# First layer's seven-product heads: softmax normalised one product later, fifth product ahead of the fourth, its weight sum by an adding load, single items

## The chip, the cores and the metric

The kernel runs on one core of a Trainium2 chip. The core has five engines that run their own queues of instructions: PE (matmuls), ACT (activations, copies, casts), DVE (elementwise work and reductions), POOL and SP, both of which also issue DMAs. The metric is the device time in us of one execution, the median of several.

## The reference

A decoder trunk of two layers over 512 tokens of width 2048, all in float32. The first layer is the sparse attention that the change is about; the second (stick-breaking attention, 16 heads) is left as it is.

```python
def _dsa_mixer(x, pos, w_in, w_out):
    h = x @ w_in
    q, k, v, g, qi, wi, ki = _split(h, A_SPLITS)
    ...
    dots = jnp.einsum('bqhd,bsd->bqhs', qib, ki)
    score = jnp.einsum('bqhs,bqh->bqs', jax.nn.relu(dots), wib)
    _, sel = lax.top_k(score, k_top)
    ...
    s = jnp.einsum('bqgrd,bqkgd->bqgrk', qg, ks) * scale
    pr = jax.nn.softmax(jnp.where(valid, s, -jnp.inf), axis=-1)
    o = jnp.einsum('bqgrk,bqkgd->bqgrd', pr, vs)
    return (o * jax.nn.silu(g)) @ w_out
```

It has 16 heads of 128 in 4 key/value groups and 16 indexer heads of 64, rope on q, k, qi and ki, and 128 selected keys per query. Each layer then does x = LayerNorm(alpha x + mixer(x)) and x = x + (p W) sigmoid(x G).

## The kernel before

**Tiles and chunks.** Activations are held transposed (features on the 128 partitions, 512 tokens along them). Weights come in chunks of 512 KB (128 x 1024). Each float32 operand is split into a high part, which ACT casts, and a low part, which DVE subtracts, and a product is made of three passes on PE: high by high, high by low, low by high. For weights these are wh (`split_w`, L370) and wl (L371); chunk c is split two steps ahead of its matmuls. There are six raw buffers and three pairs of split ones.

**Seven products.** `quads` (L210 on) makes the query and the gate of one head with seven half-width products, P1 to P7, after Strassen's scheme. Of the first layer's 16 heads, 0 to 2 are made plainly and 3 to 15 in 13 quads, numbered 0 to 12. One product is one chunk: its weights are a loaded block or a sum of blocks. A sum is made by an adding DMA from POOL's queue (`add_load`, L354) or by an add on DVE (`add_plus`, L359). Before the change P7 and P5 have adding loads, P6 and P4 have adds on DVE (P4's weights are P6's plus P2's). ACT copies partial results out of PSUM (L237 after P7, L241 after P1, L245 after P6, L273 after P3), DVE adds the others (L249 after P2, L255 after P5, L259 after P4). P6 accumulates in the bank of P1, so it starts when L241 has been done. P4 completes the head's query, P3 (of the quad before, run after the next quad's P1) its gate. The activations have forms of their own for P1 to P7; S1 and S4 are made late (`late_form`, `more_forms`), and the halves' sums come from `x_sums` during the chunks ahead of the quads.

**What sets the order.** Nothing schedules: the program's order is the order on each engine. `Kernel.run` walks the chunks; at each it splits weights of a chunk two steps ahead, runs the matmuls, then pops items from a queue (`pop`): `ch.pops` items, one by default, none after P5 and P3 in the first layer's quads. An item that is None counts as popped only where fewer than three items are left behind it. `soon` puts a function on a second list that is run at the next step, whatever `pops` is.

**Attention of the first layer.** Its items per head are, in `slots`: `turn` (rope of the query: three copies on ACT, L554 to L556; a multiplication on POOL, L557; two operations on DVE, L558 and L561; then a split, L109 and L110), `first` (value matmuls of the head before, then scores and softmax of query tiles 0 and 1), `second` (tiles 2 and 3), an empty item, and `last` (transposes of the probabilities by PE, L715, and their splits). `soft_tile` makes scores on PE (L125 to L127), mask and row maximum on DVE (L787), its negative (L789), the exponential with the row sum on ACT (L790), the reciprocal on DVE (L791) and, when both tiles of the item are so far, the normalisation on ACT (L795). The sparse selection comes before: relus of rough scores (L610) and 16 rounds on DVE (`top_rounds`), the mask (`mask_scores`) and the bias (`make_bias`) as items ahead and behind.

**The end of the stage.** The last softmaxes run as items of the output projection's chunks (`mix_out(0)`), two items a chunk in the first six.

## Time and profile before

| | us |
|---|---|
| time, median of 3 runs | 2155.71 (2153.93 to 2156.15) |
| the profiled execution's own time | 2154.26 |
| its span, first to last instruction | 2152.5 |
| PE busy | 2059.7 |
| DVE busy | 1729.5 |
| ACT busy | 1202.4 |
| POOL busy | 239.3 |
| ACT, cast of weights (L370), 552 times | 574.5 |
| DVE, subtraction for weights (L371), 552 times | 673.6 |
| DVE, sum of weights (L359), 126 times | 153.4 |

The indexer's part runs from about 100 to 279 us, quads 0 to 12 from there to 681 us, the output projection of the first layer after them. How to read the rows: a timeline row has start, duration, engine, line, operation, output<-input with shapes, and in brackets the idle time of the engine before it with what ended it. A row of waits has the total, the count and the longest. A window's row has the window, its length, the busy time of each engine with the number of instructions, the granted clock of PE, the busy share of the DMA engines and GB/s.

### The profile page before, as it was taken

How to read it: one execution, taken by the hardware profiler on the slowest of the kernel's cores; microseconds unless marked ns; L12 is line 12 of the kernel's file. 1: busy time of each engine (PE TensorE's matmuls, PEld its weight loads, DVE VectorE, ACT ScalarE, POOL GpSimd, SP SyncE). 2: the span in 40 equal slices, each digit the busy share in tenths (PEclk: the TensorE clock that was granted, in tenths of full speed). 3: DMA queues.
4: the chain of work that ended last, by engine and by line, in shares of the span. 5: the costliest groups of instructions: out<-in, count | busy, mean ns of one | idle time of the engine just before them, and what ended most of it. 6: DMA issues, size and time to landing. Idle time of an engine off the chain costs nothing. (4 is left out here: it accounts for less than half of the span.)

```text
span 2152.5 us, 33632 instructions
## 1 busy us (share of the span) xinstructions
PE 2059.7 (96%) x12808; PEld 1869.5 (87%) x12808; DVE 1729.5 (80%) x2692; ACT 1202.4 (56%) x1946; POOL 239.3 (11%) x323
## 2 busy tenths in 40 slices
PE   9988978889998899999999999999999999999999
PEld 7877868788887699889988888888888888998899
DVE  5687986667677689888788888888888888998886
ACT  4564345666666454655555555555555554546553
POOL 5201010101110000000001111111111110000000
PEclk9999999999999899999999999999999999999999
DMA  6532434435454256545745554655555574665354
GB/s 240 186 108 78 127 74 114 125 105 133 128 148 163 77 144 190 171 127 157 247 126 133 135 163 133 152 157 148 156 128 155 148 209 149 156 180 175 122 168 136
DMA packets 105905, 316.00 MB, mean 147 GB/s; under 512 B 11664, under 2 KB 16016, under 8 KB 105744
## 3 DMA queue, kind: packets, MB, share of 16 engines
q1 hardware_dynamic: 87600, 247.80, 33.1%
q0 software_dynamic: 18144, 66.07, 17.8%
q8 instruction: 100, 1.64, 0.3%
q14 instruction: 61, 0.50, 0.1%
HBM read 290.75 MB, written 23.07 MB: 146 GB/s over the span
## 5 line engine op out<-in xcount | busy, mean ns | idle before, releaser
L371 DVE TENSOR_TENSOR wl<-raw,wh 128x1024 fp32r<-128x1024 f32 (+1 forms) x552 | 673.6, 1226 | 174.1 <-ACT wh L370 173.4
L370 ACT CAST wh<-raw 128x1024 fp32r<-128x1024 f32 (+1 forms) x552 | 574.5, 1048 | 148.1 <-DVE raw L359 38.2
L201 PE MATMUL g<-f,wh 128*128 128x512 f32 x1680 | 423.7, 394 | 0.5 <-DVE f L120 0.5
L204 PE MATMUL g<-h,wh 128*128 128x256 f32 x1584 | 398.4, 288 | 19.4 <-ACT s L241 18.7
L204 PE MATMUL g<-l,wh 128*128 128x256 f32 x1584 | 396.1, 287 | 0.0
L201 PEld LDWEIGHTS g<-f,wh 128*128 128x128 f32 x1680 | 302.6, 189 | 56.4 <-DVE f L120 0.9
L204 PEld LDWEIGHTS g<-h,wh 128*128 128x128 f32 x1584 | 309.6, 195 | 22.9 <-ACT s L241 20.3
L204 PEld LDWEIGHTS g<-l,wh 128*128 128x128 f32 x1584 | 310.1, 196 | 0.8
L125 PE MATMUL g<-h,wh 128*128 128x512 f32 (+1 forms) x752 | 289.3, 385 | 5.2 <-ACT wh L370 5.2
L127 PE MATMUL g<-h,wl 128*128 128x512 f32 (+1 forms) x752 | 288.6, 384 | 2.1 <-DVE wl L371 2.1
L126 PE MATMUL g<-l,wh 128*128 128x512 f32 (+1 forms) x752 | 288.6, 384 | 0.3 <-DVE l L110 0.3
L207 PEld LDWEIGHTS g<-f,wl 128*128 128x128 f32 x1680 | 228.8, 190 | 18.4 <-DVE wl L371 2.2
L207 PE MATMUL g<-f,wl 128*128 128x256 f32 x1680 | 234.6, 282 | 0.8 <-DVE wl L371 0.8
L207 PE MATMUL g<-h,wl 128*128 128x256 f32 x1584 | 224.5, 285 | 1.9 <-DVE wl L371 1.9
L207 PEld LDWEIGHTS g<-h,wl 128*128 128x128 f32 x1584 | 206.6, 194 | 2.1 <-DVE wl L371 2.1
L125 PEld LDWEIGHTS g<-h,wh 128*128 128x128 f32 x752 | 143.4, 191 | 30.5 <-ACT wh L370 5.8
L127 PEld LDWEIGHTS g<-h,wl 128*128 128x128 f32 x752 | 143.0, 190 | 28.0 <-DVE wl L371 3.3
L126 PEld LDWEIGHTS g<-l,wh 128*128 128x128 f32 x752 | 143.1, 190 | 25.8 <-DVE l L110 0.9
L359 DVE TENSOR_TENSOR raw<-raw,raw 128x1024 f32<-128x1024 f32 x126 | 153.4, 1218 | 0.2
L280 ACT COPY s<-g 128x512 f32<-128x512 f32 x120 | 70.1, 584 | 100.9 <-PE g L207 100.8
L354 POOL DMA_DIRECT2D raw<-in_w_q_dram x60 | 53.0, 1032 | 413.3 <-issue 252.8
L109 ACT CAST h<-s 128x512 fp32r<-128x512 f32 (+1 forms) x124 | 60.4, 544 | 52.2 <-DVE s L987 38.2
(260 smaller groups left out, 2868.8 us busy)
## 6 DMA issues: line engine op xcount, KB each, us to landing
raw<-in_w_out_dram SPq DMA_DIRECT2D x64, 512.0 KB, 4.3
raw<-in_w_gate_dram SPq DMA_DIRECT2D x64, 512.0 KB, 3.8
raw<-in_w_q_dram SPq DMA_DIRECT2D x64, 512.0 KB, 4.8
raw<-in_w_q_dram POOLq DMA_DIRECT2D x60, 512.0 KB, 6.3
raw<-in_w_kv_dram SPq DMA_DIRECT2D x56, 512.0 KB, 4.4
raw<-in_w_qa_dram SPq DMA_DIRECT2D x52, 512.0 KB, 3.7
raw<-in_w_in_dram SPq DMA_DIRECT2D x45, 512.0 KB, 4.0
raw<-in_w_qa_dram POOLq DMA_DIRECT2D x26, 512.0 KB, 5.7
```

What stands on the lines that cost most here:

```text
L109: nc.scalar.copy(h[:, lo:w], src[:, lo:w])
L125: nc.tensor.matmul(out, ah, bh, start=start, stop=False)
L126: nc.tensor.matmul(out, ah, bl, start=False, stop=False)
L127: nc.tensor.matmul(out, al, bh, start=False, stop=stop)
L201: nc.tensor.matmul(ps, part(ch.h, j), x[0], start=first, stop=False, skip_group_check=True)
L204: nc.tensor.matmul(ps[:, :HALF], part(ch.h, j), x[n], start=first and n == 0, stop=False, skip_group_check=True)
L207: nc.tensor.matmul(ps[:, :HALF], part(ch.l, j), x[0][:, :HALF], start=False, stop=stop and j == last, skip_group_check=True)
L280: nc.scalar.copy(q[name], q[bank])
L354: self.nc.gpsimd.dma_start(ch.raw, ch.add, accum_op=OP.add)
L359: self.nc.vector.tensor_tensor(ch.raw, ch.raw, ch.plus.raw, op=OP.add)
L370: nc.scalar.copy(ch.h[:, i:i + w], ch.raw[:, i:i + w])
L371: nc.vector.tensor_tensor(ch.l[:, i:i + w], ch.raw[:, i:i + w], ch.h.bitcast(F32)[:, i:i + w], op=OP.subtract)
```

## The change

Six edits, all in the first layer or in code that it shares with the second.

1. In `quads`, with `late4` (first layer alone), P5 is run ahead of P4, and P4's weights are made by an adding load of the raw block onto P6's, instead of by an add on DVE.
2. Softmax: the masked scores are scaled by a negative factor and DVE takes the minimum, which the exponential uses with scale -1, so the multiplication by -1 is gone. Reciprocals and normalisation of a pair of tiles are put on `soon`, so they come after the next product (`stage_t` does them if they are still to be done).
3. Items: `slots` has [rope of this head if it is still to be done, tiles 0 and 1, tiles 2 and 3, rope of the next head, transposes]; a rope item that finds nothing to do returns False, and `pop` then goes on to the next item if three or more are left.
4. Pops: the last chunk of the keys has one pop (none before), chunks 27 and 28 one (two before), the first six output chunks one (two before). The selection's mask and bias are part of the first and last of the 16 rounds' items.
5. `x_sums` puts the split of its sum on `soon`.
6. The late forms: S4 has a tile of its own, S1 goes into the second halves of the tiles of x; S1 is made behind P1, P7 and P6 in the first layer's quads, S4 behind P5, P4 and P7.

```diff
...
         while n > 0 and self.queue and (force or self.queue[0][0] < self.now):
             fn = self.queue.pop(0)[1]
             if fn:
-                fn()
+                fn = fn() is not False
             if fn or len(self.queue) < 3:
                 n -= 1
...
-    def quads(self, sources, forms, done, copied=False, lanes=False):
+    def quads(self, sources, forms, done, copied=False, lanes=False, late4=False):
...
             q["B"] = None
         def after5(q):
-            if q["n"] == len(sources) - 1:
+            if q["n"] == len(sources) - 1 and not late4:
                 nc.scalar.copy(q["o2"][:, :HALF], q["A"][:, :HALF])
             nc.vector.tensor_tensor(q["o2"][:, HALF:], q["s17"][:, HALF:], q["A"][:, :HALF], op=OP.add)
             q["s17"] = None
         def after4(q):
             nc.vector.tensor_tensor(q["o1"][:, HALF:], q["o2"][:, :HALF], q["E"][:, :HALF], op=OP.add)
+            if q["n"] == len(sources) - 1 and late4:
+                nc.scalar.copy(q["o2"][:, :HALF], q["A"][:, :HALF])
             q["E"] = None
             done(q["n"], 0, q["o1"])
             q["o1"] = None
...
                 third(last)
             product(q, "P6", "S2", "A", False, False, after6, grown=q["P7"], plus=q["P1"])
             product(q, "P2", "A12", "B", True, True, after2, fresh=(1, c1))
-            product(q, "P4", "A22", "E", False, True, after4, grown=q["P6"], plus=q["P2"])
+            if not late4:
+                product(q, "P4", "A22", "E", False, True, after4, grown=q["P6"], plus=q["P2"])
             product(q, "P5", "S1", "A", False, False, after5, add=(0, c2), grown=q["P1"])
+            if late4:
+                product(q, "P4", "A22", "E", False, True, after4, grown=q["P6"], add=(1, c1))
...
         rope(ps, st[2], 32, lambda a: qidx.__setitem__(m, stacked(a)), col=P)
         k.defer_by(1, lambda: idx_pair(m, 3, "ss"), lambda: (idx_pair(m, 2, "ss"), idx_pair(m, 1, "so")))
         if m == 7:
-            k.defer(mask_scores)
             for r in range(0, 16):
-                k.defer(lambda: [top_rounds(b, 1) for b in range(1, NT)])
-            k.defer(make_bias)
+                k.defer(lambda r=r: (mask_scores() if not r else None, [top_rounds(b, 1) for b in range(1, NT)],
+                                     make_bias() if r == 15 else None))
...
     def tail(h, a):
         def stage_t():
+            if "normal" in a:
+                normals(a)
             a["pt"] = []
             banks = [k.ps("s") for _ in range(3)]
             where = {0: (0, 0), 1: (1, 0), 3: (1, 384), 2: (2, 0)}
...
             if h % 4 == 0:
                 v_load(h // 4)
-        def turn():
+        def turn(h):
+            a = att.get(h, ())
+            if "t" not in a:
+                return False
             if h % 4 == 0:
                 k_load(h // 4)
             rope(a.pop("t"), st[0], 64, lambda r: a.__setitem__("q", k.split(r)))
-        if h >= PLAIN_A:
-            k.defer(turn)
-        k.defer(first, second, None, last)
+        k.defer(lambda: turn(h), first, second, lambda: turn(h + 1), last)
         if h == HEADS - 1:
             k.defer(lambda: pending.pop()())
...
     def soft_tile(a, i):
         ps, n = scores(a, i)
-        pr, mx, sm = k.tt(s="pr"), k.small(), k.small()
-        nc.vector.tensor_tensor_reduce(pr[:, :n], ps[:, :n], bias[i][:, :n], scale=SCALE, scalar=GONE, op0=OP.add,
-                                       op1=OP.max, accum_out=mx)
-        nc.vector.tensor_scalar(mx, mx, -1.0, None, op0=OP.mult)
-        nc.scalar.activation(pr[:, :n], pr[:, :n], AF.Exp, bias=mx, scale=1.0, accum_out=sm)
-        nc.vector.reciprocal(sm, sm)
+        pr, mn, sm = k.tt(s="pr"), k.small(), k.small()
+        nc.vector.tensor_tensor_reduce(pr[:, :n], ps[:, :n], bias[i][:, :n], scale=-SCALE, scalar=-GONE, op0=OP.add,
+                                       op1=OP.min, accum_out=mn)
+        nc.scalar.activation(pr[:, :n], pr[:, :n], AF.Exp, bias=mn, scale=-1.0, accum_out=sm)
         a["p"][i] = pr
         def normal():
+            nc.vector.reciprocal(sm, sm)
             nc.scalar.activation(pr[:, :n], pr[:, :n], AF.Identity, scale=sm)
-        return normal
+        a.setdefault("normal", []).append(normal)
+
+    def normals(a):
+        for fn in a.pop("normal", ()):
+            fn()
     def soft_tiles(a, *tiles):
-        for fn in [soft_tile(a, i) for i in tiles]:
-            fn()
+        for i in tiles:
+            soft_tile(a, i)
+        k.soon(lambda: normals(a))
...
     for g in range(0, KV_A, 2):
         k.block(w_in, 26 + 2 * g, xs, lambda i, ps, g=g: k_done(g + i, ps))
         k.chunks[-1].pop_first = False
-        k.chunks[-1].pops = 0
     k.chunks[12].then(v_store)
     for h in range(PLAIN_A):
         k.block(w_in, 34 + 4 * h, xs, lambda i, ps, h=h: q_done_a(h, i, ps))
...
     def x_sums(j):
         a, b = xsum[j]
         sums_in_place(a, b)
-        x23[j] = k.split(a)
         xsum[j] = b
+        k.soon(lambda: x23.__setitem__(j, k.split(a)))
     def x_more(name, js):
         for j in js:
-            if j not in x14:
-                x14[j] = k.tt(F32R, "x14")
-            late_form(name, xT[2 * j], xsum[j], x14[j])
+            late_form(name, j, xT[2 * j], xsum[j], x14)
             if name == "S4":
                 xsum.pop(j)
...
     for j in range(KT // 2):
         k.chunks[10 + 2 * j].then(lambda j=j: x_pair(j))
         k.chunks[13 + 2 * j].then(lambda j=j: x_sums(j))
-    for n in (27, 28):
-        k.chunks[n].pops = 2
...
         nc.vector.scalar_tensor_tensor(a[:, lo], b[:, hi], -1.0, a[:, lo], op0=OP.mult, op1=OP.subtract)
         nc.vector.scalar_tensor_tensor(b[:, lo], a[:, lo], -1.0, b[:, lo], op0=OP.mult, op1=OP.subtract)
-    def late_form(name, tiles, b, low):
-        t, c = tiles[name == "S4"], slice(0, HALF) if name == "S4" else slice(HALF, T)
-        nc.scalar.copy(t[:, HALF:], b[:, c])
-        nc.vector.tensor_tensor(low[:, c], b[:, c], t.bitcast(F32)[:, HALF:], op=OP.subtract)
+    def late_form(name, j, tiles, b, fours):
+        lo, hi = slice(0, HALF), slice(HALF, T)
+        if name == "S4":
+            fours[j] = k.tt(F32R, "s4")
+            h, l, b = fours[j][:, lo], fours[j][:, hi], b[:, lo]
+        else:
+            h, l, b = tiles[0][:, hi], tiles[1][:, hi], b[:, hi]
+        nc.scalar.copy(h, b)
+        nc.vector.tensor_tensor(l, b, h.bitcast(F32), op=OP.subtract)
...
     def u_more(name, js):
         for j in js:
-            if j not in u14:
-                u14[j] = k.tt(F32R, "u14")
-            late_form(name, uhl[2 * j], u[2 * j + 1][0], u14[j])
+            late_form(name, j, uhl[2 * j], u[2 * j + 1][0], u14)
             if name == "S4":
                 u.pop(2 * j + 1)
-    def more_forms(qs, more):
-        for n, name in enumerate(("P1", "P7", "P6", "P2")):
-            qs[0][name].then(lambda n=n: more("S1", (2 * n, 2 * n + 1)))
-        for q, name, js in ((0, "P4", (0, 1, 2)), (0, "P5", (3, 4, 5)), (1, "P7", (6, 7))):
-            qs[q][name].then(lambda js=js: more("S4", js))
+    def more_forms(qs, more, late4=False):
+        if late4:
+            one, four = (("P1", (0, 1, 2)), ("P7", (3, 4, 5)), ("P6", (6, 7))), ("P5", "P4", "P7")
+        else:
+            one, four = [(name, (2 * n, 2 * n + 1)) for n, name in enumerate(("P1", "P7", "P6", "P2"))], ("P4", "P5", "P7")
+        for name, js in one:
+            qs[0][name].then(lambda js=js: more("S1", js))
+        for n, (name, js) in enumerate(zip(four, ((0, 1, 2), (3, 4, 5), (6, 7)))):
+            qs[n // 2][name].then(lambda js=js: more("S4", js))
...
             ch = k.chunk4(w_out[layer], 4 * b + kc, kc, outs[b], us,
                           pre=finish if n == 6 and layer == 0 else None)
             k.chunks.append(ch)
-            if not layer and n < 6:
-                ch.pops = 2
             if n in (0, 2) and layer == 1:
                 ch.then(lambda n=n: b_tail(HEADS - 1, n // 2))
             if n in (1, 5):
...
     n_q = HEADS - PLAIN_A
     qs = k.quads([((w_qa, n), (w_qa, n_q + n)) for n in range(n_q)],
-                 lambda name, j: u_form(name, j, xT, x23, x14), a_done, copied=True)
-    more_forms(qs, x_more)
+                 lambda name, j: u_form(name, j, xT, x23, x14), a_done, copied=True, late4=True)
+    more_forms(qs, x_more, True)
     for q in qs:
         for name in ("P5", "P3"):
             q[name].pops = 0
     last = qs[-1]
     last["P6"].then(lambda: (x_drop(0), u_load(range(0, 8), KEEP_A)))
     last["P2"].then(lambda: u_load(range(8, KEEP_A), KEEP_A))
-    last["P4"].then(lambda: (x_drop(1), us_ahead(0)))
-    last["P5"].then(lambda: us_ahead(1))
+    last["P5"].then(lambda: us_ahead(0))
+    last["P4"].then(lambda: (x_drop(1), us_ahead(1)))
     last["P3"].then(lambda: x_drop(2))
```

Three places where instructions move. First ACT in a steady quad, from a split of weights on. Before the change, the rope (L554 to L556 and the cast of ra, L109) reads a query that P4 of the quad before made, and the exponentials (L790) and normalisations (L795) of tiles 0 and 1 follow each other:

```order
L370 CAST wh_6414<-raw_5993 128x1024
L554 COPY rb_6446<-o_1146_6109 64x512
L555 COPY rb_6446<-o_1146_6109 64x512
L556 COPY ra_6445<-o_1146_6109 128x512
L109 CAST h_6453<-ra_6445 128x512
L370 CAST wh_6457<-raw_6202 128x1024
L790 ACT_TABLE_LOAD
L790 ACTIVATE pr_6507,s_6509<-pr_6507,s_6508 128x128
L790 ACTIVATE pr_6518,s_6520<-pr_6518,s_6519 128x256
L795 ACTIVATE pr_6507<-pr_6507,s_6509 128x128
L795 ACTIVATE pr_6518<-pr_6518,s_6520 128x256
L370 CAST wh_6527<-raw_6327 128x1024
```

After the change, from the split of P7's weights on: the normalisations of tiles 2 and 3 (L801), the split of P1's weights, the rope (L559 to L561), the cast of its result, and the split of P3's weights.

```order
L375 CAST wh_6140<-raw_5850 128x1024
L801 ACTIVATE pr_6122<-pr_6122,s_6124 128x384
L801 ACTIVATE pr_6131<-pr_6131,s_6133 128x512
L375 CAST wh_6175<-raw_5986 128x1024
L559 COPY rb_6208<-o_1162_6110 64x512
L560 COPY rb_6208<-o_1162_6110 64x512
L561 COPY ra_6207<-o_1162_6110 128x512
L109 CAST h_6215<-ra_6207 128x512
L375 CAST wh_6219<-raw_6020 128x1024
L237 COPY s_1187_6249<-g_6224 128x256
L109 CAST h_6264<-s_6251 128x512
L109 CAST h_6268<-s_6252 128x512
```

The rope moved behind P4, into the place where P3's weights are to be split, and the normalisation moved behind a split of weights (the exponentials of these two tiles stand one row ahead of the first row here). The transposes' casts (`h<-s`, three) come after P7 instead of after P6.

The second place is POOL in the steady quads. Before, there are two adding loads and one rope multiplication per quad (P7's load is the second of each pair of loads):

```order
L557 TENSOR_TENSOR rb_5460<-rb_5460,sin_198 128x512
L354 DMA raw_5341<-in_w_qa_dram 128x1024
L354 DMA raw_5546<-in_w_qa_dram 128x1024
L557 TENSOR_TENSOR rb_5786<-rb_5786,sin_198 128x512
L354 DMA raw_5667<-in_w_qa_dram 128x1024
L354 DMA raw_5872<-in_w_qa_dram 128x1024
L557 TENSOR_TENSOR rb_6116<-rb_6116,sin_198 128x512
L354 DMA raw_5993<-in_w_qa_dram 128x1024
```

After, there are three: the load for P5, the one for P4 (into a raw tile that an earlier row has loaded, that of the quad's P7 and P6), and the one for the next quad's P7 directly behind it.

```order
L562 TENSOR_TENSOR rb_5234<-rb_5234,sin_198 128x512
L359 DMA raw_5016<-in_w_qa_dram 128x1024
L359 DMA raw_4884<-in_w_qa_dram 128x1024
L359 DMA raw_5206<-in_w_qa_dram 128x1024
L562 TENSOR_TENSOR rb_5556<-rb_5556,sin_198 128x512
L359 DMA raw_5338<-in_w_qa_dram 128x1024
L359 DMA raw_5206<-in_w_qa_dram 128x1024
L359 DMA raw_5528<-in_w_qa_dram 128x1024
```

The third is ACT in the indexer: before, the cast of a sum of x (`h<-xa`) stands ahead of two relus (L610) and the casts of qi,

```order
L556 COPY ra_986<-g_808 128x384
L109 CAST h_999<-xa_830 128x512
L610 ACTIVATE relu_1009<-s_1003 128x512
L610 ACTIVATE relu_1012<-s_1004 128x512
L623 CAST qi_1016<-ra_965 64x384
L623 CAST qi_1019<-ra_965 64x384
L623 CAST qi_1023<-ra_986 64x384
L623 CAST qi_1026<-ra_986 64x384
L370 CAST wh_1029<-raw_802 128x1024
```

and after the change behind them and behind a cast of weights:

```order
L561 COPY ra_986<-g_804 128x384
L615 ACTIVATE relu_1005<-s_999 128x512
L615 ACTIVATE relu_1008<-s_1000 128x512
L628 CAST qi_1012<-ra_965 64x384
L628 CAST qi_1015<-ra_965 64x384
L628 CAST qi_1019<-ra_986 64x384
L628 CAST qi_1022<-ra_986 64x384
L375 CAST wh_1025<-raw_798 128x1024
L109 CAST h_1061<-xa_826 128x512
```

The relus wait no more for the cast ahead of them, which itself waits for DVE's sums.

More of the change, by code (lines that the diff above doesn't have):

```diff
@@ L1026, in u_form @@
             return s23[j][0][:, c], s23[j][1][:, c]
-        h, l = tiles[2 * j]
-        c, t = (hi, h) if name == "S1" else (lo, l)
-        return t[:, hi], s14[j][:, c]
+        if name == "S1":
+            return tuple(z[:, hi] for z in tiles[2 * j])
+        return s14[j][:, lo], s14[j][:, hi]
     def u_drop(what):
```

## The prediction

> **What bounds the kernel now.** I read the clock and span, the page's busy table and slices, the waits of PE, and PE's busy time stage by stage.
>
> ```profile
> core 0: 2152.5 us, clock 0.984
> PE 2059.7 (96%) x12808; PEld 1869.5 (87%) x12808; DVE 1729.5 (80%) x2692; ACT 1202.4 (56%) x1946; POOL 239.3 (11%) x323
> PE   9988978889998899999999999999999999999999
> PEclk9999999999999899999999999999999999999999
> PE s L715 <- ACT pr L795: 25.7, 10, 5.3
> PE g L204 <- ACT s L241: 18.7, 8, 3.6
> PE s L606 <- ACT relu L610: 14.7, 8, 5.1
> ```
>
> PE is the bound, but not everywhere: the slices below 9 lie in the first third (a slice is 53.8 us). The columns of a wait are total us, times, longest. Three waits hold 59 of the 93 us that PE idles, all three on ACT: the transposes on the last normalisation of the softmax (L795), P6's matmuls on the copy of P1's sum (L241), the indexer's rough scores on a relu. The windows place them (PE, PEld, DVE, ACT, POOL busy; then the clock):
>
> ```profile
> 100.00:278.70 178.70, 163.97 (x768) 139.42 (x767) 147.14 (x266) 88.00 (x151) 19.44 (x18) 0.98 0.32 103
> 278.70:340.00 61.30, 45.87 (x328) 43.00 (x327) 46.32 (x106) 33.93 (x69) 5.98 (x8) 0.94 0.39 99
> 340.00:482.00 142.00, 122.72 (x905) 117.67 (x904) 92.63 (x180) 87.72 (x156) 14.13 (x13) 0.93 0.40 107
> 482.00:681.00 199.00, 183.15 (x1413) 179.45 (x1412) 140.85 (x252) 135.45 (x232) 20.55 (x20) 0.97 0.53 147
> 681.00:745.00 64.00, 48.33 (x211) 39.94 (x210) 40.25 (x88) 32.99 (x60) 2.08 (x2) 0.87 0.29 90
> 850.00:900.00 50.00, 50.00 (x351) 1.00 0.53 170
> ```
>
> These are the indexer, quads 0 and 1, quads 2 to 5, quads 6 to 12, and the last softmaxes under the first output chunks. Behind them PE idles for nothing (50.00 of 50.00), so a us saved before 745 us is a us of the end, and nothing can be saved behind it. The waits of four windows (the two middle ones, then the last, then the second):
>
> ```profile
> PE s L715 <- ACT pr L795: 14.2, 5, 5.1
> PE g L204 <- ACT s L241: 15.1, 7, 2.4
> PE s L715 <- ACT pr L795: 5.3, 1, 5.3
> PE s L125 <- ACT h L109: 4.3, 1, 4.3
> PE g L125 <- ACT wh L370: 3.2, 1, 3.2
> PE s L715 <- ACT pr L795: 6.2, 4, 3.1
> ```
>
> **A steady quad (6 to 12).** Two periods, from P6 to P6, with PE's rows at one of these points, then rows of ACT, of DVE by form:
>
> ```profile
> 522.84:551.04 28.20, 25.54 (x203) 24.93 (x203) 19.93 (x37) 19.19 (x34) 3.07 (x3) 1.00 0.49 126
> 551.04:579.65 28.61, 26.78 (x203) 26.31 (x203) 20.14 (x37) 19.40 (x34) 3.05 (x3) 0.94 0.46 118
> 542.76 0.27 PE L204 MATMUL g<-h,wh 128*128 128x256 f32 x1
> 545.62 0.28 PE L204 MATMUL g<-l,wh 128*128 128x256 f32 x1
> 551.04 0.39 PE L204 MATMUL g<-h,wh 128*128 128x256 f32 x1 [2.38 <-ACT s L241]
> 555.50 1.25 PE L715 MATMUL s<-ident,pr 128*128 128x128 f32 x10
> 517.92 0.62 ACT L790 ACTIVATE pr<-pr,s 128x384 f32<-128x384 f32 x1 [3.34 <-DVE s L789]
> 520.37 1.21 ACT L795 ACTIVATE pr<-pr,s 128x384 f32<-128x384 f32 x2
> 521.49 1.03 ACT L370 CAST wh<-raw 128x1024 fp32r<-128x1024 f32 x1
> 529.69 0.62 ACT L554 COPY rb<-o 64x512 f32<-64x512 f32 x1
> 533.81 0.62 ACT L109 CAST h<-ra 128x512 fp32r<-128x512 f32 x1 [2.22 <-DVE ra L561]
> L371 DVE TENSOR_TENSOR wl<-raw,wh 128x1024 fp32r<-128x1024 f32 x49 | 59.9, 1223 | 29.5 <-ACT wh L370 29.2
> L359 DVE TENSOR_TENSOR raw<-raw,raw 128x1024 f32<-128x1024 f32 x14 | 17.1, 1218 | 0.0
> L789 DVE TENSOR_SCALAR s<-s 128x1 f32<-128x1 f32 x27 | 4.1, 153 | 0.9
> ```
>
> PE has 25.54 us of work in 28.20; ACT is busy for 19.19 and DVE for 19.93. None of the three is full. The period is set by a chain that goes back and forth: ACT's exponentials wait for DVE (3.34), the splits behind them come late, and the copy L241 that stands behind both comes 2.38 late. A product is 2.86 us (from the first row of P1 at 542.76 to that of P3 at 545.62).
>
> **The change, steady quads.** Removed from DVE per quad: the add for P4 (1.218) and four multiplications (4 x 0.153). As DVE has 8 us of slack, that counts only where it stands in the chain. I therefore walk the new order from P6's start at 0. Up to P3 of the next quad PE has 25.54 - 2.86 = 22.7 us of work. ACT and DVE do, in the order shown above: P6, P2 and all attention but the transposes, 2 x 2.86 + (25.54 - 7 x 2.86 - 1.25) = 10.0; the two exponentials of tiles 2 and 3 end 2 us later (from 517.92 to 520.37 it is 2.45, and the first starts before the last scores), 12.0. Then the split of P7 (1.03 + 1.22 on DVE), two sums and reciprocals (0.7), the normalisations (1.21): 16.2. The split of P1 (1.03 + 1.22), the add for P6 (1.22) and the sum of P4's output (0.4): 20.1. Only now can the rope of the next head read P4's output: first copy to cast 533.81 - 529.69 = 4.1, cast 0.6, and the split of P3's weights, which is behind that cast in ACT's queue, 1.0: 25.8. PE wants it at 22.7, so **a new wait of some 3.1 us on wh ahead of P3** takes the place of the one on L241. In the order before, the rope is behind P5 and its output had been ready since P4. Behind the waiting cast stand the next splits, hence the next products.
>
> Period: 25.54 + 3.1 = 28.6 against 28.2, **+2.8 us for seven quads**.
>
> The clock adds to it:
>
> ```profile
> 520.00:530.00 10.00, 8.13 (x69) 1.00 0.79 192
> 550.00:560.00 10.00, 8.96 (x63) 0.83 0.66 178
> ```
>
> Behind the 2.38 us wait at 551.04 the granted clock drops to 0.83 in the mean of 10 us, behind a shorter one at 522.84 it stays at 1.00. The quad with the drop takes 28.61 instead of 28.20, so a drop costs 0.4 us here, as the chain hides the rest. Three more quads with it: **+1.2**. [...]
>
> **The adding load of P4.** It is a 512 KB transfer on POOL's queue that may start only when DVE has read P6's raw weights, and ACT needs it two products later. By the same walk the release comes 0.7 us after P6's start (DVE's subtraction for P6 ends while P6 runs on its high part), and ACT reaches P4's split at 7.0 (P6 at 2.9, value matmuls and the first scores by 5.5, two short exponentials 1.5 later): an estimate of 6.3 us between them. The loads of this kind before, first the page's group, then two windows around one pair issued together:
>
> ```profile
> raw<-in_w_qa_dram POOLq DMA_DIRECT2D x26, 512.0 KB, 5.7
> raw<-in_w_qa_dram POOLq DMA_DIRECT2D x2, 512.0 KB, 7.8
> raw<-in_w_qa_dram POOLq DMA_DIRECT2D x1, 512.0 KB, 9.3
> ```
>
> The pair's middle is 7.8 and its second 9.3, so its first took 6.3. P4's load is the first of a pair in the new order (the next quad's P7 follows at once), and I take 6.3: just in time, with **+3 us** in all for the quads in which it is not. The bounds are 0 (5.7) and 3.0 per quad (9.3), 39 for 13. [...]
>
> **Quads 0 to 5.** The transposes' waits there are 6.2 and 14.2. In the new order the normalisation runs one product after the exponentials and the transposes a product or more after that, so ACT has 2.9 us or more for them: the 14.2 of quads 2 to 5 go, those of the first two quads, which follow the prologue of the pipeline, mostly stay. Back come new waits behind ropes, two of the 3.1 us kind, as the rope falls at other places in these quads: 14.2 - 6.2 = 8, with a us of the clock (0.93 in that window): **-9**. Bounds: 0, if every such wait returns (5 x 3.1 = 15.5), and -20 (14.2 and half of the early 6.2, with half of the clock's (1 - 0.93) x 142 = 9.9).
>
> **The indexer.** Its splits of the x sums stand ahead of relus in ACT's queue:
>
> ```profile
> 148.21 0.62 ACT L109 CAST h<-xa 128x512 fp32r<-128x512 f32 x1 [3.77 <-DVE xa L964]
> 175.28 0.69 PE L606 MATMUL s<-kih,qi 128*128 128x384 f32 x1 [5.14 <-ACT relu L610]
> ```
>
> ACT waits 3.77 us for DVE's sum with relus queued behind. Moving the cast a product on takes the relus out of that. But they also stand behind casts of qi that wait for the rope, and these stay. I take 6 of 14.7: **-6** (bounds -3 and -13). The top rounds are 16 items as before; two items fewer, with mask and bias merged into the first and last round, leave DVE's work as it is (0, within 2 either way, for all edits of items and pops; the late forms S1 and S4 are as many copies and subtractions as before).
>
> **The end.** In 681 to 745 us PE idles 64 - 48.33 = 15.7, and the clock at 0.87 loses 8.3 more. Single items in the output chunks, and the rope out of the way, put a product between exponentials, normalisation, transposes and value matmuls. I leave two waits of 3.1 and 2 us of clock: **-16** (bounds -10 and -23).
>
> **Sum**: +2.8 + 1.2 + 3 - 9 - 6 - 16 = -24 on the profiled execution's 2154.26 us (span 2152.5 and 1.8 around it): 2130. The median shown, 2155.71, lies 1.5 higher, by which it would be 2132. Prediction **2130**.
>
> **Rivals.** About 0.2%, 4.3 us, is what a measurement of this kernel can tell from no change.
>
> *The steady quads become bound by PE.* If the walk's late rope is wrong by 3 us, PE runs 25.9 a quad, 7 x 2.3 = 16 us less instead of 4 more: 2130 - 20 = **2110**. For it: DVE has 1.8 us less per quad, and two waits for DVE per pair of tiles leave the chain. Against: P4's output now comes last, where the rope needs it. 0.2.
>
> *The adding load comes late.* If it lands as the second of the pair did, ACT waits 3.0 us per quad, with everything behind it: 13 x 3.0 = 39 against a gain of 24 + 3 = 27, **2166**. It decides from 27 / 13 = 2.1 us late, a landing of 8.4 us from issue. For it: two of three rows are above 6.3, and the queue gets 39 such loads instead of 26. Against: the row of all 26 has 5.7. 0.1.
>
> *The gain is given back.* Every wait on a normalisation is followed by one on wh behind a rope: quads 0 to 5 gain 0, the end 10, the indexer 3, the steady quads lose 7: with the load's 3, -3, **2151**. For it: ACT idles as long as before in my walk. 0.08.
>
> **Chances.** Forecast 0.62, then 0.2, 0.1 and 0.08: faster 0.82, same 0.08, slower 0.1. The range runs from 2104, a little below the PE-bound case, to 2152, the given-back case; it leaves out the late load and some of the tails.
>
> **What would show it.** Right: no wait of the transposes on the normalisation behind quad 1; the wait of P6 on s gone, and one of some 3 us on wh ahead of P3 per quad, with the rope's cast before it on ACT; a period of 28 to 29 us; relu waits halved; the two longest waits of the last window, on a normalisation and on a cast, gone. Wrong: periods under 27 (first rival); P4's cast waiting for a DMA, with landings above 8.4 (second); a sum of PE idle before 750 us that stays at 90 (third).

## The result, and the profile after

| | before | after |
|---|---|---|
| median of 3 runs, us | 2155.71 (2153.93 to 2156.15) | 2136.03 (2135.62 to 2137.17) |
| ratio, 95% interval | | 0.9912 (0.9889 to 0.9934) |
| span of the profiled execution, us | 2152.5 | 2133.8 |
| DVE busy, us | 1729.5 | 1699.8 |

The kernel became 0.9% faster, 19.7 us by the medians and 18.7 by the spans; 2130 had been forecast. The page of the changed kernel: its span, PE's busy time and the slices of PE and of its clock.

```profile
span 2133.8 us, 33612 instructions
PE 2056.9 (96%) x12808; PEld 1870.5 (88%) x12808; DVE 1699.8 (80%) x2615; ACT 1198.5 (56%) x1946; POOL 250.3 (12%) x336
PE   9989979899898899999999999999999999999999
PEclk9999989999999999999999999999999999999999
```

The low slices are still there. The waits of PE over the whole span (total, times, longest):

```profile
PE g L204 <- ACT wh L375: 28.0, 10, 3.8
PE s L721 <- ACT pr L801: 10.0, 7, 5.0
PE s L611 <- ACT relu L615: 7.0, 3, 4.2
PE g L204 <- ACT s L241: 6.2, 2, 4.2
```

Set against the lines of before: the transposes' wait on the normalisation fell from 25.7 to 10.0 us, that on the copy L241 from 18.7 to 6.2, that on relus from 14.7 to 7.0. In their place stands one that was hardly there, 28.0 us of seven-product matmuls waiting for wh, ACT's cast of the weights (L375, before: L370).

To see where the time went, both programs are cut at the same places: the first matmul of the quads, the start of P3 in quad 6, the first matmul of the output chunks. Rows of PE's timeline, three of before and three of after, in that order (start, duration, operation, idle time ahead):

```profile
278.68 0.28 PE L204 MATMUL g<-h,wh 128*128 128x256 f32 x1
488.95 0.28 PE L204 MATMUL g<-l,wh 128*128 128x256 f32 x1
687.60 0.50 PE L125 MATMUL g<-h,wh 128*128 128x512 f32 x1 [3.17 <-ACT wh L370]
```

```profile
270.78 0.28 PE L204 MATMUL g<-h,wh 128*128 128x256 f32 x1
480.81 2.18 PE L204 MATMUL g<-s,wh 128*128 128x256 f32 x16 [2.63 <-ACT wh L375]
678.55 0.79 PE L125 MATMUL g<-h,wh 128*128 128x512 f32 x1 [3.18 <-ACT wh L375]
```

After the change P3 stands behind a wait of 2.63 us, the first of those that the forecast expected of the steady quads; before, the corresponding wait comes one product later, ahead of P6. The middle cut of after is therefore put ahead of the wait, at 478.18 us, so that both waits count to the steady quads.

| stretch | before | after | gain | forecast |
|---|---|---|---|---|
| up to the quads | 278.7 | 270.8 | 7.9 | 6 |
| quads 0 to 5 | 210.3 | 207.4 | 2.9 | 9 |
| quads 6 to 12 | 198.7 | 200.4 | -1.7 | -4, and -3 for the adding loads |
| from the first output chunk on | 1464.9 | 1455.3 | 9.7 | 16 |

Nearly all of the gain lies before the quads and behind them. The 13 quads, in which the named parts of the change stand, take 407.8 us instead of 408.9.

### The profile page after: what moved, and what is told of

Read it like the earlier page. It is cut to its first block, busy times and chain, and to the rows that moved or that the text cites. A ratio compares the mean times of both kernels' runs of the same rounds, so it can differ in the third digit from the quotient of the medians.

```text
span 2133.8 us, 33612 instructions
## 1 busy us (share of the span) xinstructions
PE 2056.9 (96%) x12808; PEld 1870.5 (88%) x12808; DVE 1699.8 (80%) x2615; ACT 1198.5 (56%) x1946; POOL 250.3 (12%) x336
## 5 line engine op out<-in xcount | busy, mean ns | idle before, releaser
L376 DVE TENSOR_TENSOR wl<-raw,wh 128x1024 fp32r<-128x1024 f32 (+1 forms) x552 | 672.8, 1225 | 207.4 <-ACT wh L375 206.9
L375 ACT CAST wh<-raw 128x1024 fp32r<-128x1024 f32 (+1 forms) x552 | 575.3, 1048 | 142.5 <-DVE raw L364 31.1
L204 PE MATMUL g<-h,wh 128*128 128x256 f32 x1584 | 396.1, 287 | 14.7 <-ACT wh L375 8.5
L364 DVE TENSOR_TENSOR raw<-raw,raw 128x1024 f32<-128x1024 f32 x113 | 137.7, 1219 | 0.2
L204 PE MATMUL g<-s,wh 128*128 128x256 f32 x528 | 72.7, 293 | 19.5 <-ACT wh L375 19.5
```

The source lines that it names most:

```text
L204: nc.tensor.matmul(ps[:, :HALF], part(ch.h, j), x[n], start=first and n == 0, stop=False, skip_group_check=True)
L364: self.nc.vector.tensor_tensor(ch.raw, ch.raw, ch.plus.raw, op=OP.add)
L375: nc.scalar.copy(ch.h[:, i:i + w], ch.raw[:, i:i + w])
L376: nc.vector.tensor_tensor(ch.l[:, i:i + w], ch.raw[:, i:i + w], ch.h.bitcast(F32)[:, i:i + w], op=OP.subtract)
```

## The experiments

All of them are the changed kernel, whose time is 2136.03, with one edit or two; each was timed with the kernel before beside it, whose median was 2154.3 to 2155.5 in the three sets. Ratios are to the kernel before. The changed kernel itself was not timed again in these sets, so a difference of a us or so from its 2136.03 says nothing.

### The cast behind the rope

In the steady quads the profile of after shows, on ACT, the chain that the forecast had walked. Rows of ACT, from the normalisations of tiles 2 and 3 to the split of P3's weights:

```profile
526.53 1.23 ACT L801 ACTIVATE pr<-pr,s 128x384 f32<-128x384 f32 x2 [1.76 <-DVE s L800]
527.67 1.03 ACT L375 CAST wh<-raw 128x1024 fp32r<-128x1024 f32 x1
531.46 0.62 ACT L559 COPY rb<-o 64x512 f32<-64x512 f32 x1 [2.76 <-DVE o L259]
532.09 0.62 ACT L560 COPY rb<-o 64x512 f32<-64x512 f32 x1
532.73 0.62 ACT L561 COPY ra<-o 128x512 f32<-128x512 f32 x1
535.46 0.62 ACT L109 CAST h<-ra 128x512 fp32r<-128x512 f32 x1 [2.10 <-DVE ra L566]
535.98 1.04 ACT L375 CAST wh<-raw 128x1024 fp32r<-128x1024 f32 x1
```

ACT stands idle for 1.76, 2.76 and 2.10 us, and the last row is the cast for which PE waits, 3.06 us ahead of P3:

```profile
537.08 3.33 PE L204 MATMUL g<-s,wh 128*128 128x256 f32 x16 [3.06 <-ACT wh L375]
```

The first run takes the cast of ra out of the way and leaves all else.

```diff
-            rope(a.pop("t"), st[0], 64, lambda r: a.__setitem__("q", k.split(r)))
+            rope(a.pop("t"), st[0], 64, lambda r: (a.__setitem__("r", r), k.soon(lambda: turned(a))))
...
+    def turned(a):
+        if "r" in a:
+            a["q"] = k.split(a.pop("r"))
```

> Edit: the changed kernel, with the split of the roped query put off by one product, so that its cast no longer stands ahead of the split of P3's weights on ACT. Theory 1 (ACT's queue: the cast of the roped query, waiting 2.1 us for DVE, holds up the weights of P3): the wait of PE on wh ahead of P3, 2.6 to 3.3 us in each steady quad, falls below 1 us, the period from 28.6 to 26.5 to 27.3 us, all waits on wh from 28 to under 12 us, and the time by 12 to 20 us to 2116 to 2124. Rival (the whole chain of ACT and DVE sets the period, the cast is only where it shows): the wait moves to another place of the quad, the period stays above 28 us and the time within 4 us of 2136.

Measured: 2116.79 us (2112.26 to 2117.94), ratio 0.9818 (0.9805 to 0.9831). A period of this kernel, and PE's row at its end:

```profile
501.47:528.24 26.77, 25.80 (x202) 24.92 (x202) 17.70 (x32) 18.99 (x34) 3.86 (x4) 1.00 0.59 148
528.24 0.39 PE L204 MATMUL g<-h,wh 128*128 128x256 f32 x1 [0.77 <-ACT s L241]
```

The period is 26.77 instead of 28.6, the wait on wh ahead of P3 is gone, and what is left is 0.77 us on L241. So the cast was the hold-up, and the rival, that the whole chain sets the period, falls: ACT does as much in a shorter period (busy for 18.99 us of 26.77 here, for 19.04 of 28.36 in the changed kernel's period from 508.72 us).

The second way out of the same place puts the rope two products later, where it was before the change:

```diff
-        k.defer(lambda: turn(h), first, second, lambda: turn(h + 1), last)
+        k.defer(lambda: turn(h), first, second, None, last)
```

> Edit: the changed kernel with the rope of a head at the head of its own items, as before the change, two products later than in the changed kernel. Theory 1 (the rope right behind P4 makes ACT wait for P4's output, 2.76 us a quad, and its cast then holds up P3's weights): without the first, periods of 26.5 to 27.8 and 2118 to 2130. Rival (the new slot brought the gain of the quads that the late normalisation ate): 2140 or more.

Measured: 2117.12 us (2115.96 to 2118.82), ratio 0.9825 (0.9812 to 0.9839). Theory 1 holds; the time is 0.9 us below its range. From the quads' start (271.55) to the first output chunk (646.62) it takes 375.1 us instead of 407.8. Of that, 14 us are lost at the end (1469.5 us from there instead of 1455.3), where the transposes now wait longer than at any place of the other kernels:

```profile
673.93 0.47 PE L721 MATMUL s<-ident,pr 128*128 128x128 f32 x1 [12.04 <-ACT pr L801]
```

### The normalisation one product later

```diff
         for i in tiles:
             soft_tile(a, i)
-        k.soon(lambda: normals(a))
+        normals(a)
```

> Edit: the changed kernel with reciprocals and normalisation right behind the exponentials of a pair of tiles, as before the change. Theory 1 (putting them off keeps PE's transposes from waiting, worth the most at the end and in the first quads): 5 to 12 us slower, 2141 to 2148, with waits of transposes on the normalisation again. Rival (putting them off only moves reciprocals behind DVE's subtraction, where ACT idles 1.76 us twice per quad): faster, by up to 13 x 3.5 less what the transposes wait: 2100 to 2133.

Measured: 2109.93 us (2108.47 to 2112.61), ratio 0.979 (0.9777 to 0.9802): 26 us faster, so my theory 1 is wrong, and the time is in the rival's range. The quads take 383.8 us (270.17 to 653.93). Two views: a steady period of this kernel, and ACT's and DVE's rows in the changed one that say why.

```profile
520.05:547.09 27.04, 25.30 (x203) 24.84 (x203) 18.18 (x32) 18.88 (x34) 3.84 (x4) 1.00 0.57 145
```

```profile
521.73 0.81 ACT L801 ACTIVATE pr<-pr,s 128x128 f32<-128x128 f32 x2 [1.76 <-DVE s L800]
520.00 1.23 DVE L376 TENSOR_TENSOR wl<-raw,wh 128x1024 fp32r<-128x1024 f32 x1 [2.09 <-ACT wh L375]
521.48 0.21 DVE L800 RECIPROCAL s<-s 128x1 f32<-128x1 f32 x2
```

A product later means behind the next split of weights: DVE's reciprocals of 0.21 us stand behind a subtraction of 1.23, and ACT, which has cast these weights just before, waits 1.76 us for them. That happens twice in a quad, ahead of the rope. Is it the reciprocals' place, or the normalisation's? One run has the roped query's split put off, and the reciprocals at once:

```diff
+        nc.vector.reciprocal(sm, sm)
+
         def normal():
-            nc.vector.reciprocal(sm, sm)
             nc.scalar.activation(pr[:, :n], pr[:, :n], AF.Identity, scale=sm)
```

> Edit: the changed kernel with the split of the roped query put off and the reciprocals at once, but the normalisation still one product later. Theory 1 (the harm of the late normalisation is that its reciprocal stands behind DVE's subtraction for the next weights, so that ACT idles 1.76 us twice a quad): within 4 us of the kernel with the normalisation at once, 2094 to 2106. Rival (the delay of ACT's normalisation is the harm): near 2116.8, the time with the late reciprocal, 2111 to 2119.

The other has it put off and all of the normalisation at once (both edits above together):

> Edit: the changed kernel with the split of the roped query put off by one product (as in the run that gave 2116.8) and the normalisation at once (as in the run that gave 2109.9). Theory 1 (two separate hold-ups of ACT's queue, the cast behind the rope 2.1 us and the two waits for late reciprocals 1.76 us each, in one chain): they add up until PE is the bound at 25.5 to 26 us a quad: 2094 to 2104. Rival (both take away the same wait ahead of P3): 2106 to 2112, no better than the normalisation alone.

Measured: 2103.45 us (2102.04 to 2105.99, ratio 0.9762, 0.9749 to 0.9776) with the reciprocals at once, 2089.13 (2088.40 to 2089.69, ratio 0.9694, 0.9681 to 0.9708) with all at once. Against the 2116.79 with both late, the reciprocals' place costs 13.3 us and the delay of the normalisation itself 14.3 more, so neither theory has the whole: 2103.45 lies in theory 1's range, but not within 4 us of the kernel with all at once. A steady period of the two kernels, 2103.45 first:

```profile
496.02:522.20 26.18, 25.41 (x203) 24.90 (x203) 18.07 (x32) 19.07 (x34) 3.86 (x4) 1.00 0.60 152
```

```profile
483.61:509.42 25.81, 25.30 (x203) 24.83 (x203) 18.00 (x32) 18.88 (x34) 3.86 (x4) 1.00 0.58 153
```

In the steady quads they differ by 0.4 us a quad, some 2.5 us for seven. Most of the rest of the 14, 12 us, lies in quads 0 to 5, whose end (the first P6 of the steady quads) comes at 469.80 us instead of 457.74. PE idles there for 21.8 us instead of 14.7; the transposes' waits for the late normalisation make 4.4 of the difference (3.44 and 2.48 us at 298.75 and 320.78 us against a single 1.54). And it is busy for 4.9 us longer, at a granted clock of 0.94 instead of 0.96. With both edits PE is busy for 25.30 of 25.81 us: here, at last, the steady quads are bound by PE, at the 25.9 us a quad that the first rival of the prediction had worked out.

### The order of P5 and P4, and the adding load

P4 first again, with its add on DVE (and the late forms S1 and S4 where they were before the change):

```diff
-                 lambda name, j: u_form(name, j, xT, x23, x14), a_done, copied=True, late4=True)
-    more_forms(qs, x_more, True)
+                 lambda name, j: u_form(name, j, xT, x23, x14), a_done, copied=True)
+    more_forms(qs, x_more)
```

> Edit: the changed kernel with P4 ahead of P5 again and P4's weights added on DVE (no late4), the rest of the change kept. Theory 1 (the rope right behind P4 holds up the next split): the rope still follows P4 directly, P5 now stands between it and the next quad, so the wait on wh ahead of P3 goes or moves to P1, with one product (2.9 us) more of cover, but DVE has 1.2 us more per quad: period 27.5 to 28.5, time 2124 to 2136. Rival (the new order of P5 and P4 with its adding load is what brought the change's gain): time 2145 or more, back towards 2155.

Measured: 2128.03 us (2127.16 to 2128.45), ratio 0.9874 (0.9861 to 0.9886), 8 us faster: theory 1. The wait on wh is shorter, about 2 us a quad (window 482 to 681 us, six of them and one of 5.4 at the first output chunk):

```profile
PE g L204 <- ACT wh L375: 11.6, 6, 2.0
PE g L125 <- ACT wh L375: 5.4, 1, 5.4
```

The load alone, with P5 still ahead:

```diff
-                product(q, "P4", "A22", "E", False, True, after4, grown=q["P6"], add=(1, c1))
+                product(q, "P4", "A22", "E", False, True, after4, grown=q["P6"], plus=q["P2"])
```

> Edit: the changed kernel with P4's weights added on DVE (1.22 us) instead of by an adding load, P5 still ahead of P4. Theory 1 (the loads land in time but for 4.4 us of waits, the add on DVE would stand in the chain of the quads): 13 x 1.2 us less the 4.4: 3 to 11 us slower than the changed kernel, 2139 to 2147. Rival (the load costs as much as it saves): within 3 us of 2136.

Measured: 2136.59 us, ratio 0.9904 (0.989 to 0.9919); its six runs fall into two lots, two at 2128.8 and 2129.0, four at 2135.5 to 2138.1. The granted clock of the whole run was 0.988 and 0.989 in the first two, 0.981 to 0.985 in the four. The median says the rival: 1.22 us of DVE per quad or a load on POOL's queue makes no difference that the runs show. And once the chain is relieved, neither counts, nor the order (the kernel of 2089.13 with P4 first and the add on DVE):

> Edit: the kernel that gave 2089 (roped query's split later, normalisation at once) with P4 ahead of P5 and P4's weights added on DVE. Theory 1 (there PE is the bound at 25.8 us a quad, so neither the order nor 1.2 us of DVE counts): within 4 us of 2089. Rival (the adding load is worth its 1.2 us a quad on DVE, the order P5, P4 too): 2095 to 2110.

Measured: 2088.76 us (2087.26 to 2091.56), ratio 0.9695 (0.9681 to 0.9708): theory 1. The places of the late forms S1 and S4 were changed only together with this order, so what they are worth alone is not known.

### The rest of the change

Single items in the output chunks, undone:

```diff
+            if not layer and n < 6:
+                ch.pops = 2
```

> Edit: the changed kernel with two items per chunk again in the first six output chunks. Theory 1 (single items brought the end's gain of 9.7 us, counted from the first output chunk): 6 to 12 us longer, 2142 to 2148, with waits of 4 to 5 us of transposes or value matmuls behind 680 us. Rival (the new place of the rope and the shorter softmax brought it): within 3 us of 2136.

Measured: 2144.70 us (2139.05 to 2145.27), ratio 0.9946 (0.9934 to 0.9959). The quads have the waits of the changed kernel and take 2.4 us longer, at a clock of 0.95 instead of 0.98 between 482 and 630 us. From the first output chunk (680.71) to the end it takes 1462.3 us instead of 1455.3, and these two waits are new:

```profile
697.22 0.80 PE L125 MATMUL o<-h,h 128*128 128x512 f32 x1 [7.89 <-ACT h L109]
718.50 2.37 PE L721 MATMUL s<-ident,pr 128*128 128x128 f32 x8 [4.04 <-ACT pr L801]
```

So theory 1 holds: 7.0 of the 9.7 us of the end are the single items. The minimum, undone:

```diff
+        nc.vector.tensor_scalar(mn, mn, -1.0, None, op0=OP.mult)
```

(with the maximum of the scores at positive scale, as before)

> Edit: the changed kernel with the row maximum and its multiplication by -1 again (64 instructions of 0.15 us on DVE, each between the maximum and the exponential). Theory 1 (they stand in the chain ACT waits for, so they count fully where it sets the period): 4 to 10 us longer, 2140 to 2146. Rival (hidden in DVE's slack): within 3 us of 2136.

Measured: 2146.72 us (2144.82 to 2148.55), ratio 0.9961 (0.9948 to 0.9973), 10.7 us longer, 0.7 above theory 1's range. The wait ahead of P3 is 3.05 to 3.15 us in six of the seven steady quads, where it was 2.6 in most, and a period is 29.8 us (483.98 to 662.48 us are six) instead of 28.6. So the instructions do stand in the chain. But that they count fully, 64 x 0.15 = 9.6 us, is not shown: in these six periods PE idles only 1.6 us longer and is busy for 5.2 us longer, for the same matmuls, at a granted clock of 0.94 instead of 0.98. The larger part came by the clock.

The split of the x sums, and the selection's items:

> Edit: the changed kernel with the split of the x sums made at once, as before the change. Theory 1 (putting this split off lets the relus go ahead and is what brought the quads' start from 278.7 to 270.8 us): start of the quads at 276 to 279 us, time 5 to 8 us longer than the changed kernel's 2136, that is 2141 to 2144, with the waits on relus back to 12 us or more (7.0 now). Rival (the merged items and single pops moved the start): start at 270 to 272, time within 2 us of 2136.

> Edit: the changed kernel with the selection's items and pops as before the change (mask and bias items of their own, no pop at the keys' last chunk, two pops at chunks 27 and 28). Theory 1 (since the later split of the x sums moved the quads' start by 1.4 us only, these items moved it by the other 6.5): start of the quads at 275 to 278 us in place of 270.8, time 2140 to 2145. Rival (neither alone, the late split and the items cover each other): start at 270 to 273, time within 3 us of 2136.

Measured: 2141.32 us (ratio 0.9934, 0.9921 to 0.9948) and 2141.35 (0.9931, 0.9917 to 0.9945), whose intervals overlap that of the changed kernel. Both times lie where theory 1 put them, and yet theory 1 is wrong in both: the quads start at 272.21 and 271.33 us, not at 275 or later. The relus wait for 8.2 us with the early split, no more than the 8.4 of two other kernels that have the late one (the one with the rope's split put off and the one with the maximum). With the early split the quads take 3.2 us longer, at a granted clock of 0.94 instead of 0.98 between 482 and 630 us. So neither edit alone moved the start of the quads by the 7.9 us that the whole change moved it; together they may (one covering for the other), and that was not run. With the selection's items the quads take 413.4 us instead of 407.8, and the waits that grew most are those of the first two heads' transposes, 9.73 us at 311.75 and 4.29 at 334.92 (5.01 and 2.51 in the changed kernel).

## Why the prediction was right, and where its steps were not

The forecast of 2130 and the range from 2104 to 2152 hold the 2136.03. Its steps:

- **A saved us before 745 us is a us of the end**: held. In the changed kernel the window from 850 to 900 us is PE's without a gap, as before.
- **Steady quads: the wait on L241 goes and one of 3.1 us on wh, behind the rope's cast, takes its place**: held in kind, and the run with the cast put off shows the mechanism. The size was somewhat too high: 2.60 to 2.66 us in five of the seven quads, 3.06 and 3.33 in two. Six periods, from P3 at 480.81 to P3 at 652.53, take 171.72 us, 28.6 each, the very number forecast, but partly by luck: the four periods at a granted clock of 1.00 take 27.9 to 28.6 us, 28.2 in the mean, and the two that begin with a drop of the clock (at 537.08 and 594.48) 29.4 each, which the forecast had as a term of its own. Before, the six from 494.38 to 664.60 took 170.22.
- **The clock, +1.2**: came in another way. Three of the seven waits are followed by a lower clock (0.66 in the 5 us from 537.08, 594.48 and 652.53, 1.00 behind the others) instead of four before, and the granted clock in the window from 482 to 681 us is 0.97, as before. But a drop costs 1.2 us of a period (29.4 against 28.2), not 0.4. That the drop goes by the length of the wait, as the forecast had read it, is wrong (last section).
- **The adding load, +3**: its landing is 5.8 us at the median of all 39, and ACT waits four times for a load:

```profile
raw<-in_w_qa_dram POOLq DMA_DIRECT2D x39, 512.0 KB, 5.8
ACT wh L375 <- DMA raw<-in_w_qa_dram: 4.4, 4, 2.5
```

  "Just in time" was right. What the 4.4 us of ACT cost PE was not separated; with the add on DVE in place of the load the time is the same (2136.59).
- **Quads 0 to 5, -9**: the step that failed, measured at -2.9. I had said that the normalisation one product later frees the transposes, and had let two new waits of 3.1 us come back. The two stretches (before first: length, busy time of the engines, then the clock), and two waits of after in the window from 340 to 482 us:

```profile
278.68:488.95 210.27, 175.56 (x1284) 167.51 (x1282) 143.64 (x293) 125.15 (x231) 21.24 (x23) 0.94 0.39 105
270.78:478.18 207.40, 178.11 (x1293) 172.13 (x1291) 130.35 (x256) 127.41 (x238) 26.51 (x29) 0.92 0.48 121
PE g L204 <- ACT wh L375: 11.1, 4, 3.8
PE s L721 <- ACT pr L801: 0.7, 2, 0.5
```

  The transposes' waits did go (14.2 us before, 0.7 after), but waits on wh took their place: 11.1 us, of which 2.63 are the first wait of the steady quads, so 8.5 instead of 6.2, with 2.0 on L241. PE idles 5.4 us less, not 8, and where a us of clock was to be gained, it is busy for 2.5 us longer, at a clock of 0.92 instead of 0.94. And the reason was wrong: with the normalisation at once, the transposes wait 1.52 us at 296.87 us and then for less than half a us in all quads, so it was not the delay that freed them. The rope's place has a part in it: with the rope in its old slot, and the normalisation still late, they wait for 4.79 us at 368.71. The new waits on wh need both the delay and the rope's cast: of the three, one of 1.37 us is left with the normalisation at once, two of 1.15 and 1.02 with the cast put off (shorter than a us not counted). The rival "the gain is given back" had named this mechanism. The far bound of the forecast for these quads is mis-added: 14.2, 3.1 and 5.0 are 22.3, not 20; no other number rests on it.
- **The indexer, -6**: measured at -7.9, but not by the mechanism I gave. The relus' waits fell by 7.7 us, but with the early split they stay low too (8.2 against 14.7). The late split alone accounts for 1.4 of the 7.9; the cause of the rest stays open.
- **The end, -16**: -9.7, of which the single items are 7.0 and the later normalisation at most 1.7 (1457.0 us from 653.93 to the end with the normalisation at once). The term was mis-sized. The same 72.4 us from the first output chunk on, before and after:

```profile
687.60:760.00 72.40, 59.90 (x248) 49.13 (x249) 48.97 (x98) 35.45 (x62) 2.08 (x2) 0.88 0.28 84
678.55:750.95 72.40, 66.35 (x315) 54.27 (x316) 55.30 (x98) 38.52 (x67) 3.90 (x4) 0.94 0.30 90
```

  I had left two waits of 3.1 us and 2 us of clock. Two of that size did stay, 3.18 us just ahead of the first output chunk and 2.82 on a cast of u at 731.48. With them stayed short ones of 3.2 us together, and a clock of 0.94, which is some 4 us by an estimate from these rows ((1 - 0.94) x 72.4).

So the sum came close by luck: two terms that were too good (quads 0 to 5 and the end, 12.4 us) and two that were too bad (the indexer, and the steady quads with their clock and loads, 7.2 us) partly met: -24 + 12.4 - 7.2 is the -18.7 of the spans but for a tenth. Undone one at a time, the parts show what was inside the 19.7: the minimum 10.7 and the single items 8.7 us of gain, in part by the clock, against 26 for the late normalisation and 19 for the rope's cast that were given away (together 45 of the 47 us between 2136.03 and 2089.13), and 8 for P5 ahead of P4, which count for nothing once the other two are gone (2088.76).

## What to carry to other kernels

ACT and DVE ran their instructions here in the program's order, so "one step later" has to be said of each engine that takes part: a normalisation on ACT was put off, and its 0.2 us reciprocal on DVE went behind a subtraction of 1.2 us for which ACT itself is needed first, and ACT idled for 1.76 us. Before an instruction that waits for another engine is put in a queue, look at what stands behind it: here a weight cast of 1 us, and PE behind that, which idled for 3.06 us ahead of P3. And a change of several parts that gains 0.9% can hold parts that cost more than that; trying them one at a time, with one undone and another put off further, gave 3.1% in all (2089.13, ratio 0.9694), the fastest of the kernels but for one within its noise.

## What the runs showed of the hardware that was not expected

Waits of one length do not always cost the same clock. Rows of P3's first 16 matmuls, each behind a wait: two of the changed kernel, two of the kernel with the maximum, two of the one with the normalisation at once.

```profile
566.52 2.18 PE L204 MATMUL g<-s,wh 128*128 128x256 f32 x16 [2.63 <-ACT wh L375]
594.48 2.84 PE L204 MATMUL g<-s,wh 128*128 128x256 f32 x16 [2.66 <-ACT wh L375]
573.31 3.78 PE L204 MATMUL g<-s,wh 128*128 128x256 f32 x16 [3.10 <-ACT wh L375]
604.20 2.18 PE L204 MATMUL g<-s,wh 128*128 128x256 f32 x16 [3.10 <-ACT wh L375]
547.09 2.18 PE L204 MATMUL g<-s,wh 128*128 128x256 f32 x16 [1.74 <-ACT wh L375]
574.17 3.61 PE L204 MATMUL g<-s,wh 128*128 128x256 f32 x16 [1.78 <-ACT wh L375]
```

After 2.63 us of idling they take 2.18 us, after 2.66 they take 2.84; the granted clock of the 5 us from there is 1.00 and 0.66. It is not a threshold between these two lengths: after 3.10 us they take 3.78 once (clock 0.50) and 2.18 another time (1.00), and even 1.78 us can be followed by 3.61 (0.66). The trace of before had it too: the forecast set a drop behind 2.38 us at 551.04 against none behind a shorter wait, but the wait at 607.80 is also 2.38 us, and the 5 us from it have a clock of 1.00, those from 551.04 one of 0.66. In the run with the x sums split at once the waits are of 2.57 to 2.67 us behind a first one of 4.02, and the clock is 0.94 in the window from 482 to 630 us, where the changed kernel had 0.98.

What decides whether the clock falls behind a wait is shown by none of these runs. The two lots of runs of the kernel with the add on DVE, 2129 and 2135 to 2138 us, had different granted clocks too (0.988 and 0.989 against 0.981 to 0.985 over the whole run), but whether that is all of their difference is open, as no trace of a run of the faster lot was taken. The kernel of 2089.13, whose steady quads have no wait of 1.7 us or more but one of 1.95 us at the end, keeps a clock of 1.00 in the window from 482 to 681 us, and its four runs lie within 1.3 us.
